# A fourth tile for the right sides read from DRAM, and all sums that collect the Strassen products on VectorE, in a two-layer diffusion backbone

## Chip, cores and metric

One core of one Trainium2 chip runs the whole program in one launch. The metric is the device time of one execution in microseconds (us), the median over several executions. Engines are named as in the profile: PE is TensorE, DVE is VectorE, ACT is ScalarE, POOL is GpSimd, and SP is the engine that issues nearly all DMAs from one queue, in order.

## What is computed

Two layers run for 1024 latent tokens and 128 context tokens that share all weights (1152 tokens, model width 1024). Every layer is a mixer followed by a squared-ReLU MLP of width 4096:

```
def sq_relu_mlp(h, w1, w2):
    return jnp.square(jax.nn.relu(h @ w1)) @ w2
...
xs = xs + ms[5] * sq_relu_mlp(modulate(xs, p['g_ffn'], ms[3], ms[4]), p['ffn_w1'], p['ffn_w2'])
```

Layer 0 mixes with a bidirectional recurrence and a pooling mixer, layer 1 with latent attention. A final RMSNorm follows. The change is in the second matrix product of the MLP (`@ w2`, 4096 to 1024), which both layers run.

## The kernel before

**Storage.** Activations lie transposed, features on the 128 partitions, tokens along the free dimension. The 1152 tokens are four chunks of 288 (`Q = 288`, `NQ = 4`); `x[c]` is the residual stream of chunk c, eight pieces of 128x288. Every matrix product is done three times over in a reduced float32 form: each operand is split into a high part (ACT, line 162) and the remainder (line 163, on DVE or POOL), and `mm3` (lines 166 to 168) sums high x high, high x low and low x high into one PSUM bank. There are eight banks (`bank()`).

**Up.** For each of 16 units of 256 hidden features, `up` (lines 754 to 769) multiplies, squares, and writes results to two DRAM buffers: `ad`, already split, and `ar`, not split.

**Down.** 14 of the 16 units are taken in seven pairs (`for s in todo[::2]`, line 845 on). Each pair is one iteration of a Strassen scheme with seven products, in the order of `LATE`: A11, A12, S3, A22, S2, S1, S4. Each product is made for two groups g = 0, 1 (two chunks each), so an iteration has 14 steps. A step is four PSUM banks of six matmuls, 24 matmuls of 288 columns.

- The left sides (weights) are combined on POOL (line 700) and split (lines 162, 163); they are ready several steps ahead.
- The right sides are of two kinds. For A11, A12 and S4 the step's tile is read ready from `ad` by `direct` (line 852, 576 KB). For S3, A22, S2 and S1 the unsplit quarter sums come into `b` (`fb_b`, line 858, two loads of 1152 KB per iteration, two buffers, one per g), POOL makes four differences or sums of each (line 696), and a split into a tile follows. The last user of `b[g]` is the split for S1. The loads of `b` for the next iteration are issued when it is through.
- All these tiles come from `next(ats)`, which before the change hands out three buffers `fq_at` in turn. A tile can be filled when the step that used the same buffer three steps earlier is done.
- SP issues in this order at the end of an iteration: four weight loads, two `fb_b` loads for the next iteration, then six `direct` loads: S4 of this iteration for g = 0 and 1, and A11 and A12 of the next for g = 0 and 1.
- Each bank is added into an accumulator `acc[name][g]` by DVE (line 881), in the first iteration copied by ACT (line 877).

**Collecting.** In the last iteration `collect` (lines 823 to 842) forms the four output blocks from the seven accumulators after each step: sums of 128x1152 in `add` (line 826), and `gated`, which scales on ACT (line 819) and adds into x on DVE (line 821). Six sums per g and layer stand in the code, not counting that of A12: S2, S3, A22 after S2, and A11, S1, S4 after S1; with A12 they are seven. Three of the seven are on DVE, four on POOL.

**Plain.** Two more units (`PLAIN`) follow without Strassen in `plain` (line 779 on), chunk after chunk, eight outputs of 12 matmuls each; DVE adds each bank into x (line 352), ACT squares x (lines 266, 269), and the squares are summed for the next norm (line 270), on POOL for the first chunks. Four outputs into the next chunk PE runs six small matmuls (line 280) that need this sum, and a little later six more (line 289) that need the reciprocals and diagonals from DVE (lines 283, 285).

**What sets the order.** PE's order is as written. ACT, DVE, POOL and SP are ordered by a scheduler with a model of the time; each runs its queue strictly in order.

Of the kernel before, what the change touches and what calls it, by code (L numbers as in the profile page):

```python
# [77 lines left out]
def emit(tc, A, O):  # L78
    nc = tc.nc
    act = nc.scalar.activation  # L80
    ve = nc.vector
    po = nc.gpsimd
# [212 lines left out]
    def modulate(norm, x, c, hs, l, ffn, lo_eng=(po, ve), inplace=False, spare=None):  # L295
        scl = (sc_ffn if ffn else sc_mix)[l]
        sh0 = 24 if ffn else 0
        hh, hl = hs[c]
        for k in range(KT):
            xn = x[c][:, k, :]  # L300
            sh = lambda g: mod[l][:, sh0 + k, g:g + 1]
            if inplace:
                for a, b, g in groups(c, norm.ch):
                    ve.tensor_scalar(xn[:, a:b], xn[:, a:b], scl[:, k, g:g + 1], sh(g), op0=OP.mult, op1=OP.add)
                split(hh[:, k, :], hl[:, k, :], xn, eng=lo_eng[k % len(lo_eng)])
                continue
            xs = spare.t([P, norm.ch], tag="xn", bufs=2)
            for a, b, g in groups(c, norm.ch):
                ve.scalar_tensor_tensor(xs[:, a:b], xn[:, a:b], scl[:, k, g:g + 1], norm.rs[c][:, a:b],
                                        op0=OP.mult, op1=OP.mult)  # L310
            for a, b, g in groups(c, norm.ch):
                act(hh[:, k, a:b], xs[:, a:b], AF.Identity, bias=sh(g))
            for a, b, g in groups(c, norm.ch):
                ve.scalar_tensor_tensor(hl[:, k, a:b], xs[:, a:b], sh(g), hh[:, k, a:b].bitcast(F32),
                                        op0=OP.add, op1=OP.subtract)
# [402 lines left out]
    def slots_of(pools):  # L718

        while True:  # L720
            for s in pools:
                h = s.t([P, 1024], F32R, tag="hlh", bufs=3 if s is state["wl"] else 2)
                lo = s.t([P, 1024], F32R, tag="hll", bufs=3 if s is state["wl"] else 2)
                for i in range(2):
                    yield h[:, i * 512:(i + 1) * 512], lo[:, i * 512:(i + 1) * 512]
# [10 lines left out]
    def cycle(*makers):  # L736
        while True:
            for f in makers:
                yield f()
# [3 lines left out]
    def ffn(l, x, hs, hclose, tail, slow, then):  # L743

        fq = Scope(f"fq{l}", side="right")
# [5 lines left out]
        four = lambda p, n=3: lambda: p.t([P, 2, 2, Q], F32R, tag="at", bufs=n)  # L751
# [54 lines left out]

        fz = Scope(f"fz{l}", side="right")
        fb = Scope(f"fb{l}")
        raws = cycle(*[from_wp] * 3, lone(fx), lone(fz))
        slots = slots_of([fw, fw, state["wl"], state["wl"], state["wl"]])  # L810
        ats = cycle(four(fq))
        ae = Each(f"acc{l}")
        acc = {n: [ae.t([P, 4, Q]) for _ in range(2)] for n in ("A11", "S3", "A22", "S2", "S1", "S4", "A12")}

        def gated(c, half, src):

            for m in range(4):
                for a, e, q in groups(c):
                    act(src[:, m, a:e], src[:, m, a:e], AF.Copy, scale=gate[:, 4 * half + m, q:q + 1])
            xv = x[c][:, 4 * half:4 * half + 4, :]  # L820
            ve.tensor_tensor(xv, xv, src, op=OP.add)

        def collect(name, g):

            t = {n: a[g] for n, a in acc.items()}
            add = lambda e, o, p, q: e.tensor_tensor(t[o], t[p], t[q], op=OP.add)  # L826
            if name == "A12":
                add(ve, "A12", "A12", "A11")
            elif name == "S3":
                gated(2 * g, 0, t["A12"])  # L830
            elif name == "S2":
                add(ve, "S2", "S2", "A11")
                add(po, "S3", "S3", "S2")
                add(po, "A22", "A22", "S3")
            elif name == "S1":
                add(po, "A11", "S3", "S1")
                add(ve, "S1", "S1", "S2")
                add(po, "S4", "S4", "S1")
                gated(2 * g, 1, t["A22"])
            elif name == "S4":  # L840
                gated(2 * g + 1, 1, t["A11"])
                gated(2 * g + 1, 0, t["S4"])

        todo = [s for s in range(ns) if s not in PLAIN]
        for s in todo[::2]:
# [15 lines left out]
            for name, o in LATE:  # L861
                ws = next(cw)
                for g in range(2):
                    if o > 2:
                        t = next(ats)
                        split(t[:, :, 0, :], t[:, :, 1, :], right[g][:, :, o - 3, :])
                    else:
                        t = begun[g] if o == 0 else direct(g, o)
                    for m in range(4):
                        b = bank()[:, :Q]  # L870
                        for j in range(2):
                            mm3(b, ws[j][0][:, m * P:(m + 1) * P], ws[j][1][:, m * P:(m + 1) * P],
                                t[:, j, 0, :], t[:, j, 1, :], j == 0, j == 1)
                        tick(0.8)
                        to = acc[name][g][:, m, :]
                        if s == todo[0]:
                            act(to, b, AF.Copy)
                        elif end and name == "S4":
                            accum(x, b, m, 2 * g + 1, gate)
                        else:  # L880
                            ve.tensor_tensor(to, b, to, op=OP.add)  # L881
                    if end:
                        collect(name, g)
        ae.close()
        fb.close()
        fp = Scope(f"fp{l}", side="right")
        then()
# [65 lines left out]
    def leave():  # L953
        ht.close()
        h0.close()

    ffn(0, x, hs, leave, Tail(nm, x, spill, lambda c, m: (po, ve)[c // 3], (5,) * 4), slow,
        lambda: hin.extend(chunk_pairs(hx, 4)))
    hs = hin
# [488 lines left out]

    end = Tail(nm, x, done, lambda c, m: ve if c == NQ - 1 else po, (5, 5, 5, 4))
    ffn(1, x, hs, leave, end, lambda *a: iter(()), lambda: None)  # L1450
    gain(NQ - 2)
    gain(NQ - 1)
# [130 lines left out]
```

## Time and profile before

| what | value |
|---|---|
| median of 3 runs | 2968.59 us (2967.73 to 2974.57) |
| profiled execution | 2964.8 us, span 2962.8 us |
| PE busy | 2791.4 us, 94% of the span |
| DVE busy | 1910.7 us, 64% |
| ACT busy | 1352.5 us, 46% |
| POOL busy | 1187.8 us, 40% |
| chain that ended last | PE 76%, DVE 9%, DMA 4%, ACT 4%, POOL 3%, issue 3% |
| in that chain | DMA fq_at<-dram_t 3%, POOL acc_t L826 1% |
| mean granted clock of PE | 0.974 of full speed |

The span runs from the first to the last instruction of the profiled execution. The chain is followed back from the last instruction to what released each step. The down part of layer 0 lies between about 880 and 1280 us of the span, that of layer 1 between about 2550 and 2950 us. PE starts a matmul before the one ahead of it has ended, so a matmul's own duration (about 0.30 us) is more than the distance between starts (0.13 us).

### The profile page before, as it was taken

The numbers are of one execution on the slowest core, as the hardware profiler recorded it, in microseconds if no ns is written. First come the engines' busy times: TensorE is split into PE (matmuls) and PEld (weight loads), VectorE is DVE, ScalarE is ACT, GpSimd is POOL, SyncE is SP. The second block draws the span as 40 slices with busy tenths as digits, with TensorE's granted clock in tenths as the row PEclk, the third lists the DMA queues.
The fourth block names the chain that finished last, engine by engine and source line by source line (L and its number), as shares of the span: only waits on it lengthen the run. The fifth ranks groups of instructions, "written<-read, shape, count | busy, mean of one in ns | idle before, by whom it ended". The sixth has DMA issues, their size and how long they took to land.

```text
span 2962.8 us, 51575 instructions
## 1 busy us (share of the span) xinstructions
PE 2791.4 (94%) x19896; PEld 2693.8 (91%) x19896; DVE 1910.7 (64%) x3518; ACT 1352.5 (46%) x3143; POOL 1187.8 (40%) x984
## 2 busy tenths in 40 slices
PE   5898799999999999899999999999999999999987
PEld 3886698999999999898999999988999999999987
DVE  5559677665656787875777777776831112377886
ACT  3356243222335222454777777773432223532335
POOL 3544111112157867624333233331011112777775
PEclk7999899999999999999999999999999999999998
DMA  5233414656655554420000000023244444555442
GB/s 225 94 120 103 167 51 166 217 207 215 219 188 175 181 172 158 136 81 21 20 15 21 14 15 23 23 91 109 85 172 156 151 163 151 187 169 173 153 158 88
DMA packets 144941, 372.78 MB, mean 126 GB/s; under 512 B 15944, under 2 KB 49080, under 8 KB 143288
## 3 DMA queue, kind: packets, MB, share of 16 engines
q1 hardware_dynamic: 144696, 369.50, 36.7%
q8 instruction: 156, 2.56, 0.4%
q14 instruction: 89, 0.73, 0.1%
HBM read 260.68 MB, written 108.75 MB: 125 GB/s over the span
## 4 chain that ended last, share of the span: by engine, by line
PE 76%; DVE 9%; DMA 4%; ACT 4%; POOL 3%; issue 3%; SPq 0%; DVEq 0%; ACTq 0%; POOLq 0%
PE ps_b L166 19%; PE ps_b L167 19%; PE ps_b L168 19%; PE pS_o L1145 3%; PE pS_t L1127 3%; DMA fq_at<-dram_t 3%; PE pS_s L166 3%; PE pS_s L168 2%; PE pS_s L167 2%; ACT aw_p L1120 1%; POOL acc_t L826 1%; PE pS_g L166 1%; PE pS_g L168 1%; PE pS_g L167 1%; ACT aw_ph L1131 1%
## 5 line engine op out<-in xcount | busy, mean ns | idle before, releaser
L765 POOL TENSOR_TENSOR fu_r<-fu_r 128x576 f32<-128x576 f32 x128 | 159.9, 1249 | 670.1 <-ACT fu_ah L764 647.3
L167 PE MATMUL ps_b<-ht_t,wl_hlh 128*128 128x288 f32 (+1 forms) x1312 | 404.9, 309 | 13.7 <-DVE ht_t L163 9.1
L166 PE MATMUL ps_b<-ht_t,wl_hlh 128*128 128x288 f32 (+1 forms) x1312 | 407.9, 311 | 7.3 <-ACT ht_t L162 5.0
L168 PE MATMUL ps_b<-ht_t,wl_hll 128*128 128x288 f32 (+1 forms) x1312 | 402.6, 307 | 0.0
L881 DVE TENSOR_TENSOR acc_t<-ps_b,acc_t 128x288 f32<-128x288 f32 x656 | 278.1, 450 | 94.6 <-PE ps_b L168 91.0
L766 DVE TENSOR_TENSOR fu_ah<-fu_r,fu_ah 128x576 fp32r<-128x576 f32 (+1 forms) x128 | 90.2, 705 | 358.9 <-POOL fu_r L765 358.9
L166 PE MATMUL ps_b<-fq_at,wl_hlh 128*128 128x288 f32 x1024 | 308.1, 301 | 12.1 <-DMA fq_at<-dram_t 12.1
L168 PE MATMUL ps_b<-fq_at,wl_hll 128*128 128x288 f32 x1024 | 305.3, 298 | 4.8 <-POOL wl_hll L163 4.8
L167 PE MATMUL ps_b<-fq_at,wl_hlh 128*128 128x288 f32 x1024 | 304.5, 297 | 0.0
L759 ACT ACTIVATE fu_r<-ps_b 128x288 f32<-128x288 f32 x256 | 103.9, 406 | 434.3 <-PE ps_b L168 431.0
L166 PEld LDWEIGHTS ps_b<-ht_t,wl_hlh 128*128 128x128 f32 x1312 | 250.0, 191 | 22.7 <-issue 5.8
L167 PEld LDWEIGHTS ps_b<-ht_t,wl_hlh 128*128 128x128 f32 x1312 | 250.4, 191 | 16.9 <-DVE ht_t L163 10.5
L162 ACT ACTIVATE wl_hlh<-w_raw 128x1024 fp32r<-128x1024 f32 (+1 forms) x161 | 137.3, 860 | 274.8 <-PE ps_b L167 230.6
L1135 DVE TENSOR_TENSOR aw_pl<-pS_t,aw_ph 128x384 fp32r<-128x384 f32 (+1 forms) x400 | 200.2, 540 | 83.0 <-ACT aw_ph L1131 77.4
L168 PEld LDWEIGHTS ps_b<-ht_t,wl_hll 128*128 128x128 f32 x1312 | 250.9, 191 | 0.0
L166 PE MATMUL ps_b<-fq_at,fw_hlh 128*128 128x288 f32 x736 | 221.7, 301 | 11.3 <-DMA fq_at<-dram_t 9.4
L1120 ACT ACTIVATE aw_p<-pS_s,aw_nb 128x384 f32<-128x384 f32 (+1 forms) x400 | 224.7, 579 | 15.2 <-DVE aw_nb L1114 14.3
L167 PE MATMUL ps_b<-fq_at,fw_hlh 128*128 128x288 f32 x736 | 220.3, 299 | 6.1 <-DVE fq_at L163 6.1
L1110 DVE TENSOR_REDUCE aw_mx<-pS_s 128x1 f32<-128x384 f32 (+1 forms) x400 | 203.3, 537 | 31.9 <-PE pS_s L168 30.7
L168 PE MATMUL ps_b<-fq_at,fw_hll 128*128 128x288 f32 x736 | 219.5, 298 | 0.0
L1131 ACT ACTIVATE aw_ph<-pS_t 128x384 fp32r<-128x384 f32 (+1 forms) x400 | 173.5, 486 | 83.7 <-PE pS_t L1127 83.4
L166 PEld LDWEIGHTS ps_b<-fq_at,wl_hlh 128*128 128x128 f32 x1024 | 196.8, 192 | 13.3 <-issue 10.9
(381 smaller groups left out, 8557.5 us busy)
## 6 DMA issues: line engine op xcount, KB each, us to landing
fq_at<-dram_t SPq DMA_DIRECT2D x96, 576.0 KB, 4.1
dram_t<-fu_ah SPq DMA_DIRECT2D x72, 576.0 KB, 2.8
w_raw<-in_ffn SPq DMA_DIRECT2D x64, 512.0 KB, 3.7
dram_t<-fu_r SPq DMA_DIRECT2D x112, 288.0 KB, 2.1
fb_b<-dram_t SPq DMA_DIRECT2D x28, 1152.0 KB
fq_at<-in_w_mod SPq DMA_DIRECT2D x128, 192.0 KB, 3.9
w_raw<-in_l_ffn_w SPq DMA_DIRECT2D x40, 512.0 KB, 4.6
w_raw<-in_w_mod SPq DMA_DIRECT2D x32, 512.0 KB, 4.2
```

The costliest lines, as they stand in the source:

```text
L162: act(hi, src, AF.Copy)
L166: mm(out, wh, hh, start=start, stop=False)
L167: mm(out, wh, hl, start=False, stop=False)
L168: mm(out, wl, hh, start=False, stop=stop)
L759: act(r[:, i ^ j, :], b[:, :Q], AF.Relu)
L765: po.tensor_tensor(r, r, r, op=OP.mult)
L766: ve.tensor_tensor(t[:, :, 1, :], r[:, :n, :], t[:, :, 0, :].bitcast(F32), op=OP.subtract)
L881: ve.tensor_tensor(to, b, to, op=OP.add)
L1110: ve.tensor_reduce(self.mx[:, i:i + 1], self.sc[i][0], axis=AX.X, op=OP.max)
L1120: act(self.pt[i][:, :w], v, AF.Exp, bias=self.nb, accum_out=lsum[:, self.h, self.blk, i:i + 1])
L1131: act(hi[g][:, :self.nks[g], j * P:(j + 1) * P], self.tp[g], AF.Copy)
L1135: ve.tensor_tensor(lo[g][s_], self.tp[g], hi[g][s_].bitcast(F32), op=OP.subtract)
```

## The change

`ats` now hands out four buffers in turn: `fq_at` three times, then one `fr_at` from a pool of its own, opened after `fb` and closed after the accumulators. The four sums in `collect` that were on POOL are issued on DVE.

```diff
@@ ffn @@
         fz = Scope(f"fz{l}", side="right")
         fb = Scope(f"fb{l}")
+        fr = Scope(f"fr{l}")
         raws = cycle(*[from_wp] * 3, lone(fx), lone(fz))
         slots = slots_of([fw, fw, state["wl"], state["wl"], state["wl"]])
-        ats = cycle(four(fq))
+        ats = cycle(*[four(fq)] * 3, four(fr, 1))
...
             elif name == "S2":
                 add(ve, "S2", "S2", "A11")
-                add(po, "S3", "S3", "S2")
-                add(po, "A22", "A22", "S3")
+                add(ve, "S3", "S3", "S2")
+                add(ve, "A22", "A22", "S3")
             elif name == "S1":
-                add(po, "A11", "S3", "S1")
+                add(ve, "A11", "S3", "S1")
                 add(ve, "S1", "S1", "S2")
-                add(po, "S4", "S4", "S1")
+                add(ve, "S4", "S4", "S1")
                 gated(2 * g, 1, t["A22"])
...
         ae.close()
+        fr.close()
         fb.close()
```

The number of instructions of each kind stays, but 16 sums (four per g and layer) go from POOL to DVE. Lines behind the new ones are one or two higher: 826 becomes 827, 881 becomes 882. The order on PE is the same, row for row, but for the names of the tiles. On the other engines the scheduler moved rows. Three places:

On DVE, the end of the second iteration of layer 0, with the splits for S1 (`fq_at<-fb_b`, the last two of the iteration; `fb_b_9074` and `9077` are g = 0, `9080` and `9083` are g = 1). In the first listing `acc_t_8479` and `acc_t_8483` are S2 of g = 0 and 1; in the second `acc_t_8478` is A22 of g = 1 and `acc_t_8482` S2 of g = 0. Before:

```order
L881 TENSOR_TENSOR acc_t_8479<-ps_b_9395,acc_t_8479 128x288
L881 TENSOR_TENSOR acc_t_8479<-ps_b_9403,acc_t_8479 128x288
L163 TENSOR_TENSOR fq_at_9470<-fb_b_9074,fq_at_9470 128x2x288
L881 TENSOR_TENSOR acc_t_8479<-ps_b_9411,acc_t_8479 128x288
L881 TENSOR_TENSOR acc_t_8479<-ps_b_9419,acc_t_8479 128x288
L881 TENSOR_TENSOR acc_t_8483<-ps_b_9430,acc_t_8483 128x288
L163 TENSOR_TENSOR fq_at_9505<-fb_b_9080,fq_at_9505 128x2x288
L881 TENSOR_TENSOR acc_t_8483<-ps_b_9438,acc_t_8483 128x288
```

With the change:

```order
L882 TENSOR_TENSOR acc_t_8478<-ps_b_9355,acc_t_8478 128x288
L163 TENSOR_TENSOR fq_at_9473<-fb_b_9077,fq_at_9473 128x2x288
L882 TENSOR_TENSOR acc_t_8478<-ps_b_9363,acc_t_8478 128x288
L882 TENSOR_TENSOR acc_t_8478<-ps_b_9371,acc_t_8478 128x288
L882 TENSOR_TENSOR acc_t_8478<-ps_b_9379,acc_t_8478 128x288
L882 TENSOR_TENSOR acc_t_8482<-ps_b_9398,acc_t_8482 128x288
L882 TENSOR_TENSOR acc_t_8482<-ps_b_9406,acc_t_8482 128x288
L163 TENSOR_TENSOR fq_at_9508<-fb_b_9083,fq_at_9508 128x2x288
L882 TENSOR_TENSOR acc_t_8482<-ps_b_9414,acc_t_8482 128x288
```

The split for S1 of g = 0 stands five accumulator sums earlier than before, that of g = 1 three.

On DVE, the last iteration of layer 0 where A12 is collected (line 826, now 827) while the splits for S3 and A22 are due (`fb_b_11844` and `11847` are g = 0). Before:

```order
L826 TENSOR_TENSOR acc_t_8503<-acc_t_8503,acc_t_8455 128x1152
L881 TENSOR_TENSOR acc_t_8507<-ps_b_11969,acc_t_8507 128x288
L163 TENSOR_TENSOR fq_at_12050<-fb_b_11850,fq_at_12050 128x2x288
L881 TENSOR_TENSOR acc_t_8507<-ps_b_11977,acc_t_8507 128x288
...
L821 TENSOR_TENSOR x_t_2348<-x_t_2348,acc_t_8503 128x1152
L826 TENSOR_TENSOR acc_t_8507<-acc_t_8507,acc_t_8459 128x1152
L881 TENSOR_TENSOR acc_t_8463<-ps_b_12021,acc_t_8463 128x288
L881 TENSOR_TENSOR acc_t_8463<-ps_b_12029,acc_t_8463 128x288
L163 TENSOR_TENSOR fq_at_12096<-fb_b_11844,fq_at_12096 128x2x288
```

With the change:

```order
L827 TENSOR_TENSOR acc_t_8506<-acc_t_8506,acc_t_8458 128x1152
L882 TENSOR_TENSOR acc_t_8510<-ps_b_11972,acc_t_8510 128x288
L163 TENSOR_TENSOR fq_at_12099<-fb_b_11847,fq_at_12099 128x2x288
L882 TENSOR_TENSOR acc_t_8510<-ps_b_11980,acc_t_8510 128x288
...
L822 TENSOR_TENSOR x_t_2348<-x_t_2348,acc_t_8506 128x1152
L827 TENSOR_TENSOR acc_t_8510<-acc_t_8510,acc_t_8462 128x1152
L882 TENSOR_TENSOR acc_t_8466<-ps_b_12024,acc_t_8466 128x288
L882 TENSOR_TENSOR acc_t_8466<-ps_b_12032,acc_t_8466 128x288
L163 TENSOR_TENSOR fr_at_12134<-fb_b_11853,fr_at_12134 128x2x288
```

The split for A22 of g = 0 (`fq_at_12096`, now `fq_at_12099`) stood behind both long sums and now stands behind the first of them; behind the second stands the split for A22 of g = 1.

On DVE, a little later in the same iteration, where the sums after S2 stand now (accumulators `8466` and `8470` are S3, `8474` A22, `8482` and `8486` S2, `8490` and `8494` S1):

```order
L827 TENSOR_TENSOR acc_t_8466<-acc_t_8466,acc_t_8482 128x1152
L882 TENSOR_TENSOR acc_t_8490<-ps_b_12272,acc_t_8490 128x288
L827 TENSOR_TENSOR acc_t_8486<-acc_t_8486,acc_t_8462 128x1152
L882 TENSOR_TENSOR acc_t_8490<-ps_b_12280,acc_t_8490 128x288
L882 TENSOR_TENSOR acc_t_8490<-ps_b_12288,acc_t_8490 128x288
L882 TENSOR_TENSOR acc_t_8494<-ps_b_12307,acc_t_8494 128x288
L827 TENSOR_TENSOR acc_t_8474<-acc_t_8474,acc_t_8466 128x1152
L882 TENSOR_TENSOR acc_t_8494<-ps_b_12315,acc_t_8494 128x288
L882 TENSOR_TENSOR acc_t_8494<-ps_b_12323,acc_t_8494 128x288
L827 TENSOR_TENSOR acc_t_8470<-acc_t_8470,acc_t_8486 128x1152
```

Of these four, those that write `8466`, `8474` and `8470` were on POOL; the one that writes `8486` was on DVE already. Further down, of the sums of line 352 that plain makes for its first chunk, the eighth has three sums of 128x1152 and four of its own kind behind it in the queue before the reciprocal of line 283; the order before had one of 128x1152 and four of its own kind there.

## Rows read from the trace of the kernel before

**Rows 1.** Source line 852, who waited (us, times): window 930:1160, then 2600:2850

```profile
  PE ps_b L166: 11.0, 5
...
  PE ps_b L166: 9.7, 5
```

**Rows 2.** Timeline, layer 0, second iteration (start us, us): DVE, SP's queue, PE

```profile
955.55 1.77 DVE L163 TENSOR_TENSOR fq_at<-fb_b,fq_at 128x576 fp32r<-128x576 f32 x1
...
958.34 0.74 DVE L163 TENSOR_TENSOR fq_at<-fb_b,fq_at 128x576 fp32r<-128x576 f32 x1
...
957.35 2.14 SPq L858 DMA_DIRECT2D fb_b<-dram_t  x2
959.93 18.21 SPq L852 DMA_DIRECT2D fq_at<-dram_t  x6
...
967.98 0.38 PE L166 MATMUL ps_b<-fq_at,wl_hlh 128*128 128x288 f32 x1 [1.74 <-DMA fq_at<-dram_t]
```

**Rows 3.** Windows: us, busy PE, PEld, DVE, ACT, POOL, then PEclk, DMA share, GB/s

```profile
963.00:966.00 3.00, 3.00 (x25) 3.00 (x23) 1.83 (x4) 0.00 (x0) 2.50 (x2) 1.00 1.00 406
968.00:1012.00 44.00, 44.00 (x333) 44.00 (x334) 35.08 (x68) 12.19 (x20) 33.82 (x24) 1.00 0.49 159
1015.50:1019.50 4.00, 4.00 (x21) 4.00 (x20) 1.37 (x3) 0.00 (x0) 4.00 (x4) 0.57 0.22 83
...
1189.50:1193.50 4.00, 4.00 (x21) 4.00 (x20) 4.00 (x8) 1.55 (x3) 1.49 (x1) 0.57 0.02 4
...
1246.50:1251.50 5.00, 5.00 (x22) 5.00 (x23) 1.90 (x5) 1.03 (x3) 1.92 (x3) 0.51 0.01 3
...
2912.50:2917.50 5.00, 5.00 (x23) 5.00 (x23) 1.31 (x5) 2.53 (x6) 2.06 (x3) 0.54 0.01 3
```

**Rows 4.** Waits of PE, 1160:1290, and one timeline row (us in total, times, longest)

```profile
PE ps_b L167 <- DVE fq_at L163: 3.0, 1, 3.0
PE ps_b L168 <- POOL wl_hll L163: 1.7, 1, 1.7
...
1245.52 1.12 PE L280 MATMUL ps_b<-const_t,nt_acc 128*96 128x1 f32 x6 [5.85 <-POOL nt_acc L270]
```

**Rows 5.** The same of PE in layer 1, 2840:2963

```profile
PE ps_b L167 <- DVE fq_at L163: 3.2, 1, 3.2
PE ps_b L168 <- POOL wl_hll L163: 3.0, 1, 3.0
...
2911.38 1.12 PE L280 MATMUL ps_b<-const_t,nt_acc 128*96 128x1 f32 x6 [3.65 <-POOL nt_acc L270]
```

**Rows 6.** Source line 826: duration ns min/median/max, first and last start us

```profile
L826 DVE TENSOR_TENSOR acc_t<-acc_t,acc_t x12: 1344/2433/3401, 1177.8 to 2896.1; 128x1152 f32<-128x1152 f32 x12
```

**Rows 7.** DVE's lines by form, 1205:1246 (busy us, mean ns | idle before), one timeline row

```profile
L821 DVE TENSOR_TENSOR x_t<-x_t,acc_t 128x1152 f32<-128x1152 f32 x6 | 15.4, 2573 | 0.1
...
L826 DVE TENSOR_TENSOR acc_t<-acc_t,acc_t 128x1152 f32<-128x1152 f32 x3 | 7.0, 2348 | 0.3 <-POOL acc_t L826 0.3
L163 DVE TENSOR_TENSOR wl_hll<-w_raw,wl_hlh 128x1024 fp32r<-128x1024 f32 x1 | 3.7, 3655 | 0.0
...
1286.36 1.22 DVE L163 TENSOR_TENSOR wl_hll<-w_raw,wl_hlh 128x1024 fp32r<-128x1024 f32 x1
```

**Rows 8.** DVE's lines by form in layer 1, 2872:2911

```profile
L821 DVE TENSOR_TENSOR x_t<-x_t,acc_t 128x1152 f32<-128x1152 f32 x6 | 14.2, 2367 | 0.1
L826 DVE TENSOR_TENSOR acc_t<-acc_t,acc_t 128x1152 f32<-128x1152 f32 x3 | 8.9, 2970 | 0.3 <-POOL acc_t L826 0.3
```

**Rows 9.** Timeline, behind the last long sums: DVE, ACT, POOL in layer 0, DVE in layer 1

```profile
1243.01 1.35 DVE L352 SCALAR_TENSOR_TENSOR x_t<-ps_b,const_t,x_t 128x288 f32<-128x288 f32 x3
...
1245.50 0.44 ACT L269 ACTIVATE nt_sq<-x_t 128x288 f32<-128x288 f32 x1 [0.42 <-POOL nt_acc L270]
...
1247.41 0.80 POOL L270 TENSOR_TENSOR nt_acc<-nt_acc,nt_sq 128x288 f32<-128x288 f32 x1 [0.32 <-ACT nt_sq L269]
...
2907.99 1.36 DVE L352 SCALAR_TENSOR_TENSOR x_t<-ps_b,const_t,x_t 128x288 f32<-128x288 f32 x3
```

## Prediction

> **What bounds the kernel now.** PE is busy for 94% of the span, so I looked for the places where it stands still or runs slowly, in this order: the chain of waits, PE's waits by line, the windows with the granted clock, the timelines around each place, and DVE's groups by form. A difference of 0.3%, 8.9 us, is about what a measurement can tell from no change. The profiled execution is 3.8 us shorter than the median; the sum is made against its 2964.8 us and then moved to the median of 2968.6.
>
> In the down part PE is gapless for most of an iteration: 333 matmuls start in 44.0 us at full clock [rows 3], 0.132 us each, so a step of 24 matmuls takes 3.17 us and a bank of six 0.79 us. Two kinds of place break this.
>
> *First, S4's tile.* In five iterations of each layer PE waits for a tile that line 852 loads, 11.0 us in one layer and 9.7 us in the other [rows 1], 2.1 us each time. The timeline shows one such place, and why. DVE's splits for S1, the last users of `b`, run at 955.55 to 957.32 and at 958.34 to 959.08. SP issues the first of the next two `fb_b` loads at 957.35, behind the first split, the second behind the other, and the loads of line 852 only from 959.93. PE starts S4 of g = 0 at 967.98, after 1.74 us without a matmul [rows 2]. While these loads run the DMA engines are full (share 1.00, 406 GB/s) [rows 3]. So three things precede the wait: the tile's buffer comes free, the splits for S1, and SP's order.
>
> After five of these ten waits PE runs about 4 us at its lower clock: four times at 0.57 of full speed, of which one is shown, and once at 0.62 [rows 3]. 4 x 4 x 0.43 + 4 x 0.38 = 8.4 us are lost. **Term A**, the waits and what follows them, is 11.0 + 9.7 + 8.4 = 29.1 us.
>
> *Second, the end of each down part.* Where the sums are collected and plain begins, PE waits for a split on DVE (3.0 and 3.2 us), for a weight split on POOL (1.7 and 3.0) and for the summed squares of plain's first chunk (5.8 and 3.6) [rows 4, 5]: 20.3 us. Five stretches at half clock stand behind these waits, the first, the third and the last of them shown [rows 3]; together they lose 1.7 + 1.7 + 2.5 + 2.9 + 2.3 = 11.1 us. At most 31.4 us are to be had here.
>
> The cause of the last wait is a full DVE. From 1205 to 1246 it has next to no idle time [rows 7], and a sum of 128x1152 takes 1.34 us at the least but 2.43 at the median and 3.40 at the longest [rows 6]. POOL is at work on its own long sums in the same time. The split of 128x1024 shows the same: 3.66 us there, 1.22 us at 1286 where POOL has no long sum [rows 7].
>
> **The change, part by part.**
>
> *The fourth tile.* A step's tile may be filled when the step four back is done, one step (3.17 us) sooner. The order of DVE shows the split for S1 of g = 0 five accumulator sums earlier and that of g = 1 three; at one per 0.79 us that is about 3.9 and 2.4 us. SP's order is unchanged here, so its load for S4 follows the later of the two and is issued at about 957.5 instead of 959.93; if it takes the same 8.05 us from issue to first use [rows 2], it is there at 965.5. PE would want it at 967.98 - 1.74 = 966.2. The bounds are nothing gained (the loads share full DMA engines and land no sooner) and all of A. I take all: everything ahead moves by 2.4 us or more, the mean wait is 2.1, and with the wait its half clock goes. Where single waits are longer than 2.4 us a few tenths stay; that is inside the range. Next in line are the splits for A22 of the following iteration, which need the `fb_b` loads; these also start 2.4 us sooner, so they are covered.
>
> *The sixteen sums.* POOL loses eight long sums per layer. DVE gains eight, and without POOL beside it I price each at the shortest row, 1.34 us [rows 6]: 10.7 us more per layer. The other end is 3.40. In return the DVE work of the end gets shorter. In layer 0 six sums of line 821 fall from 15.4 to 8.0, three of line 826 from 7.0 to 4.0, the split from 3.7 to 1.2 [rows 7]: 12.9 us saved, net 2.2 us less DVE work. In layer 1 it is 14.2 to 8.0 and 8.9 to 4.0 [rows 8], 11.1 us, net 0.4 less. So DVE does the same work in about the same time, and what matters is where in its queue the eighth sum of plain's first chunk stands. It now has three long and four short sums behind it: 3 x 1.34 + 4 x 0.45 = 5.8 us. The queue ended at 1243.01 + 1.35 = 1244.4 and 2909.4 [rows 9]. Less 2.2 and 5.8 the eighth sum ends at 1236.4; less 0.4 and 5.8 in layer 1, at 2903.2. Behind it come a square on ACT, 0.44, and an add on POOL, 0.80 [rows 9], with 0.2 for the two handovers: PE's line 280 can start at 1237.8 and 2904.6, and not at 1245.52 and 2911.38 [rows 4, 5], 7.7 and 6.8 us sooner. POOL's adds used to trail because POOL had long sums ahead of them; it has none now. With the wait goes its half clock, 2.5 and 2.3 us [rows 3]. Against this, the reciprocal of line 283 now stands behind those 5.8 us, and PE's line 289 waits for it, about 2 us by the distance between the two lines. Net 8.2 and 7.1, **15.3 us**. The waits of lines 167 and 168 ahead are contained in this: PE cannot pass line 280 sooner than DVE lets it.
>
> The Trainium skill, page "SBUF — State Buffer", section "Who interferes with whom", says that a DVE instruction with two SBUF inputs contends with a GpSimd instruction that reads SBUF, and that the shared ports are an exclusive lock for a whole instruction. The stretched sums agree in kind; in size only in part, since the longest is 3.40 us and not 1.34 plus a whole POOL sum. This speaks against the change, as the long sums of DVE now stand beside POOL's adds of squares: if the add on the path waited for one whole DVE sum, 1.34 us per layer, the sum would be 41.7 us in place of 44.4, and the time 2926.9.
>
> *The rest.* PE's order is the same. POOL's remaining work has fewer sums in its way. Sum: 29.1 + 15.3 = **44.4 us**; 2964.8 - 44.4 = 2920.4 on the profiled execution, 2924.2 on the median.
>
> **The rivals.**
>
> 1. *DVE takes the end's gain back.* Its queue is full where the sums land, and one bank waits on DVE every 0.79 us. If the long sums stay near their median beside POOL's adds and splits, the waits at the ends keep their size and only A remains: 2968.6 - 29.1 = **2939.5**. For it: the small net of 2.2 and 0.4 us. Against it: POOL loses its long sums, beside which the stretched sums stood.
>
> 2. *The fourth tile starts nothing sooner.* The loads share full DMA engines (406 GB/s [rows 3]); if S4's tile lands when the two `fb_b` loads let it, an earlier issue gains nothing, and only the ends do: 2968.6 - 15.3 = **2953.3**. Against it: the whole burst starts with the first split, and this one stands five sums earlier. This is also the case in which the change does not do what it says.
>
> 3. *Slower.* A long sum on DVE stops the banks behind it, and PE with them through eight banks. Sixteen new sums at the longest row, 3.40 us [rows 6], are 54.4 us; if each stop also brings a stretch like that at 1189.5, 1.7 us [rows 3], 81.6 us. From this go A's 29.1, and POOL's waits with the half clock behind them, 5.8 + 3.6 + 1.7 + 3.0 + 9.4 = 23.5: slower by 29.0, **2997.6**. It decides from (29.1 + 23.5 + 8.9) / 16 = 3.8 us of PE time per sum without the lower clock. Against it: eight banks hold 8 x 0.79 = 6.3 us of PE's work, more than one sum and what is queued with it.
>
> **How the numbers follow.** The forecast has a chance of 0.72, rival 1 of 0.18, rival 2 of 0.06, rival 3 of 0.04. The predicted time is that of the forecast, 2924. The lower end is all that either kind of place loses, 29.1 + 31.4 = 60.5 us: 2908. The upper end takes in rival 1, 2939.5, and some 2 us of leftovers: 2942; rivals 2 and 3 lie outside. Faster by over 0.3%: the forecast, rivals 1 and 2 but for the runs of the last that come short, 0.93; no change 0.04; slower 0.03.
>
> **What the changed profile would show.** A right: line 852 has no answers from PE in the two windows, or tenths, and no half clock in the middle of the down parts; the splits for S1 end 2 to 4 us further ahead of S4's first matmul. Wrong: the same 2 us waits, with DMA share 1.00 ahead of them. The ends right: the 128x1152 sums on DVE close to 1.34 us, and line 280's waits gone or under 1 us, with some 2 us on line 289. Wrong: sums still at 2.4 us, and PE waiting for splits behind them. I would be wrong upwards if PE waits for DVE at the splits of S3 and A22, where long sums stand ahead of them, and downwards if line 289 finds its reciprocal ready.

## Result and profile after

The changed kernel takes 2927.4 us, the median of four runs (2925.8 to 2933.0), beside 2970.3 for the kernel before in the same comparison: a ratio of 0.9858, 95% interval 0.9839 to 0.9876. That is 42 us less, or 37 to 48. Predicted were 2924 us and 44.4 us less. A second comparison, in experiment 5, gave 0.9859.

The profiled execution is the longest of the four, 2933.0 us, 5.6 above the median. Against the profile before it loses 5.7 us in layer 1's attention, which the change does not touch. Between line 289's last matmuls ahead of it and the next line 280, PE took 717.9 us before and 723.7 now, and the granted clock is lower in three windows there. The columns are those of [rows 3]; the windows of 30 us from 1363 to 2113 that are not shown stand at 1.00. In the kernel before the same work stands 22 us later; cut in the same way, the first window (1385 to 1415) had 0.83 there and all others 1.00, so the three cost 30 x (0.06 + 0.06 + 0.06) = 5.4 us.

```profile
1363.00:1393.00 30.00, 22.34 (x124) 20.87 (x125) 21.82 (x49) 18.79 (x52) 14.88 (x16) 0.77 0.04 14
...
1723.00:1753.00 30.00, 27.56 (x189) 26.55 (x188) 21.41 (x53) 20.52 (x62) 11.26 (x14) 0.94 0.08 22
...
1903.00:1933.00 30.00, 28.68 (x193) 27.61 (x194) 21.46 (x51) 22.20 (x68) 10.51 (x17) 0.94 0.15 43
```

So the sum is made stage by stage. From line 289 of the fourth chunk's norm ahead of an MLP to line 289 of plain's first chunk, layer 0 is 22.6 us shorter and layer 1 17.1; another 0.4 comes a chunk later in layer 0: 40.1 us in all.

**The fourth tile.** PE's waits in the changed kernel, over the whole of layer 0's down part and then of layer 1's (us in total, times, longest):

```profile
PE ps_b L280 <- POOL nt_acc L270: 6.3, 1, 6.3
PE ps_b L166 <- DVE acc_t L882: 1.9, 2, 1.7
PE ps_b L289 <- DVE nt_acc L285: 0.6, 1, 0.6
PE ps_b L166 <- DVE x_t L352: 0.6, 1, 0.6
...
PE ps_b L280 <- POOL nt_acc L270: 5.2, 1, 5.2
PE ps_b L280 <- DVE nt_acc L270: 3.3, 1, 3.3
PE ps_b L166 <- DVE acc_t L882: 2.5, 3, 1.7
PE ps_b L289 <- DVE nt_acc L285: 1.0, 1, 1.0
PE ps_b L166 <- DVE x_t L352: 0.6, 1, 0.6
PE ps_b L166 <- DMA fq_at<-dram_t: 0.3, 1, 0.3
```

The ten waits of [rows 1] are gone but for 0.3 us, and no line of a split stands here any more. The windows of the two down parts say the same: PE is busy in 280.00 of 280 us and in 259.70 of 260, at a clock of 1.00.

```profile
880.00:1160.00 280.00, 280.00 (x2119) 279.88 (x2118) 209.77 (x374) 103.37 (x197) 237.72 (x161) 1.00 0.55 180
2540.00:2800.00 260.00, 259.70 (x1964) 259.50 (x1964) 198.02 (x351) 97.37 (x186) 218.67 (x148) 1.00 0.56 184
1226.00:1230.00 4.00, 4.00 (x21) 4.00 (x22) 3.50 (x7) 1.61 (x5) 2.93 (x3) 0.64 0.00 0
2879.50:2884.50 5.00, 5.00 (x23) 5.00 (x23) 2.33 (x6) 3.96 (x11) 3.37 (x4) 0.52 0.01 2
```

The last two rows are what is left of the lower clock at the ends, 4 x 0.36 + 5 x 0.48 = 3.8 us where it was 11.1. The timeline of the iteration of [rows 2]: the splits for S1 on DVE, SP's queue, and PE's first matmul of S4.

```profile
952.41 0.74 DVE L163 TENSOR_TENSOR fq_at<-fb_b,fq_at 128x576 fp32r<-128x576 f32 x1
...
956.04 1.10 DVE L163 TENSOR_TENSOR fq_at<-fb_b,fq_at 128x576 fp32r<-128x576 f32 x1
...
953.18 4.37 SPq L859 DMA_DIRECT2D fb_b<-dram_t  x2
957.66 0.41 SPq L853 DMA_DIRECT2D fq_at<-dram_t  x1
...
966.66 0.37 PE L166 MATMUL ps_b<-fq_at,wl_hlh 128*128 128x288 f32 x1
```

The second split ends at 957.14, SP issues S4's load at 957.66, and PE takes the tile at 966.66 with no idle time in the row's brackets.

**The sums.** All 28 sums of 128x1152 are on DVE and take 1.36 us at the median, where the twelve of before took 2.43 [rows 6]. Yet line 280 waits 6.3 and 5.2 us, longer than the 5.85 and 3.65 of [rows 4, 5]. The chain of waits through layer 0's end shows how (start, us, what):

```profile
1216.64 1.46 DVE acc_t L827
1218.13 0.44 ACT acc_t L820
1218.58 1.37 ACT acc_t L820 x3
1219.95 0.34 ACT nt_sq L269
...
1220.42 0.80 POOL nt_acc L270
1221.30 1.80 POOL nt_acc L270
1223.16 1.80 POOL nt_acc L270
1225.01 1.12 PE ps_b L280 x6
```

A long sum on DVE releases four scalings on ACT; a square that was ready stands behind them in ACT's queue; then POOL makes three adds in a row, the first in 0.80 us, the other two in 1.80. The DVE rows of the same time, with the eighth sum of plain's first chunk as the second of line 352:

```profile
1219.90 0.93 DVE L352 SCALAR_TENSOR_TENSOR x_t<-ps_b,const_t,x_t 128x288 f32<-128x288 f32 x2
1220.76 1.68 DVE L827 TENSOR_TENSOR acc_t<-acc_t,acc_t 128x1152 f32<-128x1152 f32 x1
1222.36 1.94 DVE L822 TENSOR_TENSOR x_t<-x_t,acc_t 128x1152 f32<-128x1152 f32 x1
```

It ends at 1220.83, and line 280 starts 4.2 us later. In layer 1 it is 2873.96 and 2878.14, 4.2 us too.

Read side by side, the two listings show DVE and POOL taking turns. POOL's first add ends at 1221.22; the DVE sum that started beside it ends 1.22 us later, at 1222.44; POOL's second add ends 0.66 behind that, at 1223.10; the next DVE sum 1.20 behind that, at 1224.30; the third add 0.66 behind that, at 1224.96. A sum or an add that finds the other engine's running does its own work when that one has ended, so its duration grows by the rest of it: the two adds of 1.80 us carry 1.0 us of waiting each. The short sums of line 352, with one input in PSUM, show no such stretch: the second of the two at 1219.90 runs beside the first add, which takes its 0.80. The trace before shows the same, with long sums on both engines:

```profile
1229.62 2.98 DVE L821 TENSOR_TENSOR x_t<-x_t,acc_t 128x1152 f32<-128x1152 f32 x1
1231.35 1.92 POOL L270 TENSOR_TENSOR nt_acc<-nt_acc,nt_sq 128x288 f32<-128x288 f32 x1
1232.96 1.53 DVE L826 TENSOR_TENSOR acc_t<-acc_t,acc_t 128x1152 f32<-128x1152 f32 x1
1234.57 2.68 POOL L826 TENSOR_TENSOR acc_t<-acc_t,acc_t 128x1152 f32<-128x1152 f32 x1 [1.29 <-DVE acc_t L826]
1235.27 3.19 DVE L821 TENSOR_TENSOR x_t<-x_t,acc_t 128x1152 f32<-128x1152 f32 x1
```

The add ends 0.67 us behind the first DVE sum (1233.27 and 1232.60), the second DVE sum 1.22 behind the add, the third 1.21 behind POOL's long sum (1238.46 and 1237.25).

### The profile page after: what moved, and what is told of

It is laid out like the page before. It is cut to its first block, busy times and chain, and to the rows that moved or that the text cites. A ratio compares the mean times of both kernels' runs of the same rounds, so it can differ in the third digit from the quotient of the medians.

```text
span 2931.0 us, 51557 instructions
## 1 busy us (share of the span) xinstructions
PE 2781.7 (95%) x19896; PEld 2685.8 (92%) x19896; DVE 1896.3 (65%) x3534; ACT 1354.9 (46%) x3143; POOL 1155.2 (39%) x968
## 4 chain that ended last, share of the span: by engine, by line
PE 77%; DVE 12%; ACT 4%; issue 3%; DMA 2%; POOL 2%; SPq 0%; DVEq 0%; ACTq 0%; POOLq 0%
PE ps_b L166 19%; PE ps_b L167 19%; PE ps_b L168 19%; PE pS_t L1129 3%; PE pS_o L1147 3%; PE pS_s L166 3%; PE pS_s L168 2%; PE pS_s L167 2%; ACT aw_p L1122 1%; PE pS_g L166 1%; PE pS_g L168 1%; PE pS_g L167 1%; DVE x_t L352 1%; DVE acc_t L827 1%; ACT aw_ph L1133 1%
## 5 line engine op out<-in xcount | busy, mean ns | idle before, releaser
L882 DVE TENSOR_TENSOR acc_t<-ps_b,acc_t 128x288 f32<-128x288 f32 x656 | 269.8, 448 | 51.0 <-PE ps_b L168 49.3
L166 PE MATMUL ps_b<-fq_at,wl_hlh 128*128 128x288 f32 x800 | 238.0, 298 | 1.6 <-DVE acc_t L882 1.1
L168 PE MATMUL ps_b<-fq_at,wl_hll 128*128 128x288 f32 x800 | 235.4, 294 | 0.0
L167 PE MATMUL ps_b<-fq_at,wl_hlh 128*128 128x288 f32 x800 | 234.8, 293 | 0.0
L163 DVE TENSOR_TENSOR wl_hll<-w_raw,wl_hlh 128x1024 fp32r<-128x1024 f32 (+1 forms) x109 | 139.4, 1279 | 99.9 <-ACT wl_hlh L162 98.7
L696 POOL TENSOR_TENSOR fb_b<-fb_b 128x576 f32<-128x576 f32 x112 | 176.6, 1588 | 25.5 <-DMA fb_b<-dram_t 21.6
L166 PE MATMUL ps_b<-fq_at,fw_hlh 128*128 128x288 f32 x576 | 172.0, 299 | 4.6 <-DVE acc_t L882 3.3
L167 PE MATMUL ps_b<-fq_at,fw_hlh 128*128 128x288 f32 x576 | 170.0, 295 | 0.0
```

The lines of the kernel that those rows point to most:

```text
L163: eng.tensor_tensor(lo, src, hi.bitcast(F32), op=OP.subtract)
L166: mm(out, wh, hh, start=start, stop=False)
L167: mm(out, wh, hl, start=False, stop=False)
L168: mm(out, wl, hh, start=False, stop=stop)
L696: po.tensor_tensor(a[:, :, o, :], a[:, :, p, :], a[:, :, q, :], op=op)
```

## Experiments

Ratios are to the kernel before on the same chip, with 95% intervals.

**1. The parts apart.** The fourth tile alone:

```diff
-        ats = cycle(four(fq))
+        ats = cycle(*[four(fq)] * 3, four(fr, 1))
```

> Only the fourth tile; the sums stay on VectorE and GpSimd as before. My theory: the waits for S4's tile and the half clock behind them go by the tile alone, 29 to 30 us: about 2939 us, a ratio of 0.990 to the kernel before; line 853 (852 before) is answered by PE with under 1 us per layer, and the ends keep waits of 12 to 17 us. Rival: S4's load starts sooner only because the sums changed VectorE's order; then the ten waits of 2 us stay and the time is above 2960 us.

Measured 2938.8 us, 0.9898 (0.9873 to 0.9923): 30 us less. PE has 1.0 us of waits for DMA in layer 1 and none in layer 0, and no lower clock in the middle of the down parts. At the end of layer 0 it waits more than before:

```profile
PE ps_b L280 <- POOL nt_acc L270: 8.4, 1, 8.4
PE ps_b L166 <- DVE acc_t L882: 3.5, 2, 2.7
```

In layer 1 these are 5.9 and 3.5 us. So the ends keep 21.3 us in these two kinds of wait, not the 12 to 17 expected. The waits for splits are gone here too, with POOL's sums where they were, but line 280 and the banks take back as much.

The sums alone:

```diff
-                add(po, "S3", "S3", "S2")
+                add(ve, "S3", "S3", "S2")
```

and so for A22, A11 and S4.

> Only the sums on VectorE; three tiles as before. My theory: the ten waits for S4's tile stay (about 21 us with 8 us of half clock), the long sums on VectorE fall to 1.34 to 1.5 us, the waits for splits at the ends go, the wait for the summed squares stays, and the time falls by 10 to 12 us: about 2958 us, a ratio of 0.996. Rival: where PE stands for S4's tile anyway VectorE has time to catch up, so the sums alone give under 5 us: above 2964 us.

Measured 2959.9 us, 0.9963 (0.9948 to 0.9978): 11 us less. Layer 0's down part keeps the waits for S4's tile (layer 1's are 12.8 us as well, 25.6 in all where about 21 were expected):

```profile
PE ps_b L166 <- DMA fq_at<-dram_t: 12.8, 6, 3.1
PE ps_b L280 <- POOL nt_acc L270: 6.1, 1, 6.1
PE ps_b L167 <- DVE fq_at L163: 1.9, 1, 1.9
```

The sums of 128x1152 stand at 1.35 us in the median, so the absence of POOL's long sums makes them short, with three tiles as with four. The rivals of both runs fall: the parts add within their intervals, 1.02% and 0.37% make 1.39%, and 1.42% was measured for both. How the gain divides between them is known to some us only: the interval of the tile alone is 23 to 38 us. The split's wait of 1.9 us that stays here is gone with the fourth tile.

**2. Why S4's load was late.** Three tiles, but each half of the next `b` is loaded only when S4's tile of the same group is there:

```diff
+                        if name == "S4":
+                            act(junk, right[g][:, 0, 0, 0:1], AF.Copy, scale=t[:, 0, 0, 0:1].bitcast(F32))
```

> The kernel before with three tiles, but each half of the next unsplit right sides is loaded only when S4's tile of the same group has landed (a one-column read on ScalarE holds the buffer). If S4's load is late because it shares full DMA engines with those two loads, it now takes 4 to 5 us instead of 8, and PE's ten waits at S4 go (21 us); the loads of A11 or the splits of S3 may then be late instead. If it is late because its buffer comes free too late, the waits at S4 stay at about 2 us each. The theory with the prediction needs both, a late buffer and a shared burst, and so expects the waits at S4 to fall below 0.5 us each, and up to 2 us per iteration back at A11.

Measured 2999.0 us, 1.0096 (1.0074 to 1.0117), slower. In the second iteration SP issues the loads for S4 from 967.26, ACT's read shows the first landed at 971.30, and PE's next waits for a DMA are at 981.01 and 985.41, for the two tiles of A11, two steps and three behind S4's first. PE wanted S4's tile at about 981.01 - 1.1 - 2 x 3.17 = 973.6, 6.3 us behind the issue, as far as in the kernel before (966.2 - 959.93):

```profile
967.26 3.55 SPq L853 DMA_DIRECT2D fq_at<-dram_t  x2
...
971.30 0.29 ACT L871 ACTIVATE fb_junk<-fb_b,fq_at 128x1 f32<-128x1 f32 x1 [3.02 <-DMA fq_at<-dram_t]
...
981.01 0.37 PE L166 MATMUL ps_b<-fq_at,wl_hlh 128*128 128x288 f32 x1 [1.10 <-DMA fq_at<-dram_t]
985.41 0.37 PE L166 MATMUL ps_b<-fq_at,wl_hlh 128*128 128x288 f32 x1 [1.01 <-DMA fq_at<-dram_t]
```

So with three tiles, and no `fb_b` load ahead, S4's load takes 4.0 us instead of 8.05 and is in time. The two `fb_b` loads ahead were necessary for the wait; the buffer's late release alone was not enough. Whether S4's load was slow because it shared the engines with them or because it stood behind them is not told apart here. At S4 PE waits only in the last iteration, 1.6 and 1.5 us in the two layers. The price is what was late next: A11's tiles, now in the burst, the splits of the right sides behind the later `b` (waits of 9.4 us for ACT and 5.9 for DVE in layer 0), and where plain begins one wait of 6.8 us for a weight split on POOL, 6.6 in layer 1; why this one grew was not followed up. The fourth tile does not take the burst apart, it starts it sooner.

**3. The wait at line 280.** Its norm placed later in PE's order, 11 instead of 5 us of PE's work behind the first chunk's last output:

```diff
-(po, ve)[c // 3], (5,) * 4)
+(po, ve)[c // 3], (11, 5, 5, 5))
```

> The changed kernel, with the six small matmuls of line 280 for plain's first chunk placed 11 instead of 5 us of PE's work after its last output. My theory: the wait for the summed squares is late by POOL's three adds of 1.5 us and by VectorE's queue, and PE has other work to do meanwhile; the waits of 6.3 and 5.2 us and some 3 us of half clock go, and the time is 2913 to 2918 us. Rival: VectorE is the bound there, so PE stops at a bank instead, and the gain is under 5 us: above 2922 us.

Measured 2919.5 us, 0.9830 (0.9806 to 0.9853). Both waits of the first chunk's line 280 are gone; layer 0 has a wait of 1.7 us at line 289 in their place, with half clock behind it. 8 us less than the changed kernel: less than my theory asked, more than its rival.

> The changed kernel, with the norm of plain's first chunk later in PE's order: line 280 after 9 instead of 5 us of PE's work, line 289 another 4.5 instead of 1.8 us behind it. Theory: both the wait for the squares and that for the reciprocal have then passed; 11.5 us of waits and some 3 us of half clock go, the waits of e3 at line 289 (1.7 us and its half clock) too: 2913 to 2917 us. Rival: VectorE's queue is the bound, and PE stops at a bank instead: 2920 us or more.

Measured 2922.7 us, 0.9845 (0.9831 to 0.9860): line 280 waits 3.2 and 2.0 us, line 289 hardly. The time is the rival's, its cause is not: PE waits 2.3 and 0.8 us at the accumulators' banks, where the changed kernel has 1.9 and 2.5. Neither expectation holds whole.

> The changed kernel with line 280 of plain's first chunk after 11 and line 289 another 4.5 us of PE's work behind it. In e3 (11 and 1.8) a wait of 1.7 us at line 289 with half clock stayed, in e6 (9 and 4.5) waits of 3.2 and 2.0 at line 280; with both late none of them should stay: 2914 to 2919 us. Rival: VectorE is the bound behind it, and PE stops at a bank for as long: 2921 us or more.

Measured 2923.0 us, 0.9837 (0.9822 to 0.9853): line 280 waits 0.6 and nothing, but line 289 waits again, 2.3 and 3.7 us over several chunks, with half clock behind the longest. The time is the rival's again; PE waits for DVE, as the rival said, but at line 289 and not at a bank. The waits of the first chunk are partly paid later, by the norms of the next chunks, which need DVE too. Each of the three placements lies below the changed kernel's 0.9858 and 0.9859, by 0.13 to 0.29%; their intervals overlap with its own, so a gain is likely, and its size is not settled.

> Only the fourth tile, with the sums as in the kernel before, and the norm of plain's first chunk as late as in e6. If the sums on VectorE pay only by the wait at line 280, this equals e6 (2913 to 2917 us). If they pay by the waits for splits and banks and by VectorE's shorter queue, this is 6 to 11 us above e6: 2921 to 2926 us. I expect the second, since the fourth tile alone left 2.8 us twice at banks and longer waits at line 280.

This run has the fourth tile alone with the norm as late as in e6: 2932.0 us, 0.9879 (0.9864 to 0.9894). It is 9 us above e6, where 6 to 11 were expected, though both lie higher than I said. The sums on DVE pay also when line 280 stands later: at banks PE waits 4.3 and 5.7 us here, 2.3 and 0.8 in e6, while line 280 still waits 4.6 and 2.8 us here, 3.2 and 2.0 in e6.

**4. What holds line 280 back, POOL's adds or DVE's queue.** The first chunk's squares summed on DVE:

```diff
-(po, ve)[c // 3], (5,) * 4)
+(ve, po, po, ve)[c], (5,) * 4)
```

> The changed kernel, with the squares of plain's first chunk summed on VectorE instead of GpSimd (seven adds of 128x288 per layer). Theory: the wait of line 280 comes from GpSimd's three adds in a row, 1.5 us each beside VectorE's sums, where 0.45 us is what one takes on VectorE; the wait falls from 6.3 and 5.2 us to 3 to 4 us each, some 4 to 6 us in all: 2921 to 2924 us. Rival: VectorE's queue sets the wait, and seven more adds lengthen it; the wait stays or grows, and the time is 2927 us or more.

Measured 2933.1 us, 0.9885 (0.9869 to 0.9902), and the wait in layer 0 grew from 6.3 to 9.4 us:

```profile
PE ps_b L280 <- DVE nt_acc L270: 9.4, 1, 9.4
```

In layer 1 it grew from 5.2 to 8.4. The adds took 0.45 us each there, a quarter of POOL's 1.80, and the long sums beside them 1.34 or 1.35, with no add of POOL in their way. Still it is worse, and by the place of the adds in the queue more than by their length: in layer 0 the eighth sum ends at 1215.53 and line 280 starts at 1224.25, 8.7 us later, with three long and four short sums among the adds on DVE:

```profile
1214.60 0.93 DVE L352 SCALAR_TENSOR_TENSOR x_t<-ps_b,const_t,x_t 128x288 f32<-128x288 f32 x2
...
1222.06 2.13 DVE L270 TENSOR_TENSOR nt_acc<-nt_acc,nt_sq 128x288 f32<-128x288 f32 x4
...
1224.25 1.12 PE L280 MATMUL ps_b<-const_t,nt_acc 128*96 128x1 f32 x6 [9.39 <-DVE nt_acc L270]
```

The rival holds.

> The changed kernel with the two moved sums behind S1 (A11 and S4) back on GpSimd, eight in all; those behind S2 stay on VectorE. Theory: GpSimd's long sums then stand beside VectorE's in the last stretch and stretch them and the adds of squares again; the wait at line 280 grows by 1 to 2 us per layer, and the time lies between the changed kernel and the fourth tile alone: 2930 to 2936 us. Rival: VectorE's queue is what counts, and four sums less per layer, 5.4 us, shorten it: below 2925 us.

The sums A11 and S4 back on POOL: 2939.6 us, 0.9901 (0.9886 to 0.9916), as slow as the fourth tile alone. The longest sum on DVE is 3.10 us again, waits at line 280 are 5.8 and 5.7 us, and banks wait 4.4 and 4.6 us in the two layers. The time moved as the theory said, past its range, but not for its reason: line 280's waits did not grow by 1 to 2 us per layer (they were 6.3 and 5.2); those at banks did, from 1.9 and 2.5 us. Half of the sums moved shows no gain over none here.

**5. Taking sums out of DVE's queue.** The sums of g = 1 behind S2, S1 and S4 made to wait for the first chunk's reciprocal:

```diff
+            s2 = acc["S2"][1][:Q // 3, 0, 0:1]
+            ve.scalar_tensor_tensor(s2, tail.norm.col[:, 0:1], 0.0, s2, op0=OP.mult, op1=OP.add)
+            for name in ("S2", "S1", "S4"):
+                collect(name, 1)
```

> The changed kernel, with the six sums and three gated sums of group g = 1 that follow S2, S1 and S4 held back until the reciprocal of plain's first chunk is made (a one-column sum with a factor of zero makes them depend on it). Nothing is left out: they write chunks 2 and 3, which plain reaches one chunk later. Theory from e5: VectorE's queue ahead of the eighth sum sets the wait at line 280; nine sums of 1.35 us leave it, 12 us, so the waits of 6.3 and 5.2 us and their 3 us of half clock go, and some bank waits before them: 2911 to 2917 us. Rival: the sums only move, and PE waits for VectorE in the second and third chunk for as long: 2925 us or more.

> The changed kernel as it is, on the same chip as the run with the sums held back, so that the two stand side by side: 2926 to 2929 us, a ratio of 0.985 to 0.987 to the kernel before.

The first gave 2956.8 us, 0.9953 (0.9935 to 0.9972), for a reason of its own: to keep the accumulators open I had opened their pools first, and PE then waited for the first tile of each down part.

```profile
PE ps_b L166 <- DMA fr_at<-dram_t: 11.5, 1, 11.5
```

The changed kernel beside it gave 2930.0 us, 0.9859 (0.9837 to 0.9881), as expected.

> As in e9, the sums of group g = 1 behind S2, S1 and S4 wait for the reciprocal of plain's first chunk, but the accumulators lie where they did, so the 11.7 us per layer that PE waited in e9 for the first tile of the down part are gone; plain's first two chunks use the four tiles of the down part. Theory: the wait at line 280 in the first chunk goes and 3 to 6 us of it come back in the second chunk, where the held sums run: 2920 to 2926 us. Rival one: all of the 11.5 us and their half clock are won: 2911 to 2917 us. Rival two: the sums only move: 2927 us or more.

With the pools in their old order, and plain's first four tiles from the ring of the down part: 2927.1 us, 0.9851 (0.9836 to 0.9867), the same as the changed kernel. The wait of 11.5 us is gone, as it should be if the order of the pools caused it. The first chunk's line 280 waits no longer in either layer, and in layer 0 others take its place in the second chunk (line 290 here is line 289 elsewhere):

```profile
PE ps_b L290 <- DVE nt_acc L286: 3.1, 2, 2.7
PE ps_b L280 <- POOL nt_acc L270: 2.5, 1, 2.5
```

In layer 1 it is 3.8 us at the second chunk's line 280. Rival two, the sums only move, is nearest: relative to the changed kernel layer 0 lost all of what it had won (6.5 us at the first norm, 8.5 given back by the third), layer 1 kept some 3 us. That the first chunk's wait goes shows that the sums of g = 1 cause it. They leave three places at once: DVE's queue ahead of the eighth sum, ACT's queue with their scalings, and the stretch behind the eighth sum where POOL's adds take turns with them. How the wait divides between the three is not shown.

## Why the prediction was right

**Term A** was right in size and cause. 11.0 + 9.7 us of waits and 8.4 of half clock were to go; 20.4 and 8.4 went, and the tile alone gave 30 us (interval 23 to 38) beside the 29.1 of the sum. The steps hold one by one: S4's load was to be issued at 957.5 and was at 957.66; the split for S1 of g = 1 ended 9.5 us ahead of S4's first matmul, where it had been 7.1 ahead of the time at which PE wanted it, so 2.4 us sooner as worked out. That the wait needs two things, a burst and a late start, was argued then; that it goes without the burst ahead is shown by e4, and that it goes with an earlier start by e1. Rival 2 falls by e1.

**The ends** gave about 11 us and not 15.3: 11 by e2, and 40.1 - 28.8 = 11.3 by the stages. Of their steps these hold:

- The long sums take 1.34 us once POOL has none: median 1.36, and 1.35 with three tiles.
- The eighth sum was put at 1236.4 in the time of the profile before. It ended at 1220.83; the changed program starts 1.2 us later, and layer 0's part of A, 11.0 + 3 x 1.72 = 16.2, lies ahead: 1220.83 - 1.2 + 16.2 = 1235.8, 0.6 off.

The step that failed is the next: "a square on ACT, 0.44, and an add on POOL, 0.80, with 0.2 for the two handovers", 1.4 us from the eighth sum to line 280. It measured 4.2 in both layers. I had priced one square and one add as if each found its engine free. The chain shows a square behind four scalings on ACT, and three adds on POOL in a row, two of them 1.80 us long beside DVE's long sums. That is 2 x 2.8 = 5.6 us. Of each 2.8 us, 2.0 are the two adds that waited for a DVE sum, which the prediction named as speaking against the change and left out of its sum; 0.8 are the places in ACT's and POOL's queues. The trace before held a warning: there the eighth sum of layer 0 (the first of the two below) ended at about 1240.8 and line 280 started at 1245.52, 4.7 us later; in layer 1 it was 5.0 us.

```profile
1237.20 9.89 POOL L270 TENSOR_TENSOR nt_acc<-nt_acc,nt_sq 128x288 f32<-128x288 f32 x8
...
1240.27 0.93 DVE L352 SCALAR_TENSOR_TENSOR x_t<-ps_b,const_t,x_t 128x288 f32<-128x288 f32 x2
```

"POOL's adds used to trail because POOL had long sums ahead of them" took this away whole. But POOL's last long sum had ended at 1237.25, and the eight adds behind it took 1.24 us each and not 0.80, beside DVE's sums; and DVE's sums stayed.

Against the 5.6 us the 2 us per layer at line 289 did not come, since line 280 came later: 4 us back. And with line 280 still waiting, its half clock did not go: 3.8 us stayed. 15.3 - 5.6 + 4 - 3.8 = 9.9, near the 11.3 of the stages. What the ends did give is 7.3 us of half clock and the waits for splits, 3.0 + 1.7 + 3.2 + 3.0 = 10.9 us, less 5.6 at banks (1.9 + 0.6 + 2.5 + 0.6) and 2.0 more at line 280: 10.6 us.

The prediction's test for the ends, "line 280's waits gone or under 1 us, with some 2 us on line 289", therefore failed, while its time was nearly right. That is in part luck: 5.6 and 3.8 us too much stand against 4 too little. Rival 1 is half of what happened: the wait at line 280 stayed, but by POOL's adds and ACT's queue behind DVE, and the waits for splits went all the same. Rival 3 falls: no new sum took more than 2.45 us, and banks wait 5.6 us in both layers together, not 54.

The sentence on the Trainium skill (page "SBUF — State Buffer", section "Who interferes with whom") gave 41.7 us for the sum, with an add that waits for one DVE sum per layer. 42 was measured, with an interval that also holds 44.4, so the time does not choose. The rows do, and the trace agrees with the rule: the turns of 1220.42 to 1224.96 are what an exclusive lock for a whole instruction would give. An add of 0.80 us took 1.80 twice while DVE's sums beside it took 1.68 and 1.94 in place of 1.34; the added 1.0 us is what was left of the DVE sum that the add found running. Two adds per layer wait so, not one. The prediction read the longest sum before, 3.40 us, as less than a lock would make it; but that sum started at 2896.14 beside a POOL sum already running, which ended at 2898.33, and it ended 1.21 us behind that, so it does not speak against the rule.

## What to carry to other kernels

A tile in a ring can cost a wait although its load is short: look for the burst that it lands in and for what releases both; one more buffer starts the whole burst sooner, where taking the load out of the burst only made others late. When work moves off an engine that takes turns with another, price the moved work at its undisturbed duration where nothing on the other engine is left beside it, and follow the path to its end: what stays there (here POOL's adds, 1.0 us of waiting in each of two) and each queue behind (here ACT's scalings) needs its own place in the sum, not the duration of one free instruction. A wait that is pushed out of the way on one chunk tends to return on the next while the engine behind it is full; measure it before counting it as won.

## What was not expected

Moving half of the sums showed no gain: 0.9901 with eight of sixteen back on POOL, 0.9898 with all of them there. Seven adds of 0.45 us on DVE in place of adds of up to 1.80 us on POOL made PE wait 3.1 us longer. And an unchanged stage, layer 1's attention, differed by 5.7 us between two profiled executions, by the lower clock in three windows; so a stage's own difference says more than that of two spans.
